# Output projection's second half starts on weights already on chip, chunk norms of the down projection get a PSUM bank, convolution state stored in one piece

## The chip, the cores and the metric

The kernel runs on one core of a Trainium2 chip. A core has five engines that run their own instruction queues and wait for each other through semaphores: TensorE (PE, matrix products into eight PSUM banks), VectorE (DVE), ScalarE (ACT), GpSimd (POOL) and SyncE (SP, which here only issues DMAs; ACT issues some too). The metric is the device time of one launch in microseconds, the median of several runs.

## The reference, cut to what matters

One layer of a streaming encoder on 1024 prompt frames and 8 x 16 sample frames, 1152 columns in the kernel, all in fp32:

```
mix = concat(hgrn2(h), mla(h))          # h: modulated RMSNorm of x
x2  = x + gate1 * (mix @ w_out)         # output projection, 1024 -> 1024
h2  = rmsnorm(x2) * (1 + scale2) + shift2
a, v = split(h2 @ w_up)                 # two branches of D_FF = 2816
a   = causal_conv3(a)                   # its last two rows per sequence: new_state_ffn_conv
x3  = x2 + gate2 * ((gelu(a) * v) @ w_down)
y   = rmsnorm(x3) * gain
```

scale, shift and gate come from a conditioning vector: one for the prompt's columns, one per sequence for the 128 sample columns.

## The kernel before

Activations lie transposed: 128 channels on the partitions, frames along the free axis. Where full fp32 is wanted, a product is made of three (`mm3`, L293 to L295) from a rounded part and a rest of each operand; the rounding is an ACT copy (L288) and the rest a DVE subtraction (L289).

The program is written phase by phase, but a scheduler (the Tile framework) fixes each engine's order at build time by priorities, and adds the semaphore waits. Buffers are named slabs: `B0` to `B11` (128 x 1152 fp32), `W` (128 x 1024, weights), `U` (split parts), each waiting for its last reader when it is written again. `mm` and `bg` are tags of four PSUM banks each. Background pieces of work are generators in a list; `step(n)` advances them by n steps, so their instructions are placed between those of the phase in front.

*Output projection* (`proj_out`). The 1152 columns are two halves (hf) of 576. In each half eight blocks d of 128 output channels are computed in two column pieces c of 288. A piece is 24 products into one `mm` bank, in a half 384 products. The bank is read by `residual`: L1362 adds gate times product to x for the prompt columns; L1365 and L1366 do it for the 128 sample columns, which lie in the second piece of the second half. x comes by L1273 into a slab that holds blocks k and k + 4 side by side; in both halves these are `B4` to `B7`. The weights of a block come by `out_weights`: a load on SP (L1244), the rounding on ACT (L1246), the rest on DVE (L1247, 7/8 of the columns) and POOL (L1248, 1/8), into one of two slots that alternate. In the queue of blocks 0 to 7 stands twice. Then x2 is stored, its squares (L1284) are summed on DVE (L1286, tile `st`).

*Second norm* (`norm2`, once for each half). Two products with ones (L1308) give the sums, L299 to L303 1/sqrt; L1322 multiplies each slab; ACT scales and shifts the prompt columns (L1328); L1331 and L1332 do so for the sample columns on DVE. From the results seven forms (FB11, FB21 ...) are made by subtractions and split, which `up_pair` multiplies: seven products of halves in place of eight. The first norm runs beside the second half of the projection, the second after it.

*Up* (`ffn`, `up_pair`). 22 pairs j with 168 products (L1445) each. ACT (L1448, L1486) and DVE (L1453, L1481) take the banks, e is the gate branch, v the other, and their product g goes to DRAM (gd, L1519). The convolution state of each pair is collected by POOL in `sout` and `tail` and stored by two DMAs on ACT's queue (L1423, L1424).

*Down* (`down`). Three column pieces (704:1152, 256:704, 0:256). In each, all eight d accumulate in all eight banks over 22 j; weights (L1540) and g (L1546) are loaded in 11 steps jp and split. For the last steps d runs outside: then come `residual`, the square (L1575), the sum (L1577). `final` makes the last norm of a piece in the background: the product with ones (L1601) into an `mm` bank, L1602, L299 to L303, the multiplications on POOL (L1609) and DVE (L1611), and the store of y. It yields before it asks for the bank, and all banks are taken by the next piece.

Of the kernel before, what the change touches and what calls it, by code (L numbers as in the profile page):

```python
# [12 lines left out]
F32 = mybir.dt.float32  # L13
# [184 lines left out]
class Layer:  # L198
# [1006 lines left out]
    def phase_c(self):  # L1205
        nc = self.nc
        self.mla_in()
        soft, turned = None, None
        for pr in range(2):
            K, V = self.keys(pr)  # L1210
            if pr == 1:
                self.bg.append(self.sample_mla())
            for i in range(2):
                h = 2 * pr + i
                for pj in range(4):
                    Ps = self.scores(h, pj, K[i])
                    if turned:
                        self.values(*turned)
                    turned = soft and (soft[0], soft[1], self.weights_t(soft[1], soft[2]), soft[3])
                    soft = (h, pj, Ps, V)  # L1220
                    self.step(2)
        self.values(*turned)
        self.queue, self.ahead, self.n_out = list(range(KT)) * 2, [], 0
        self.out_weights()
        self.values(soft[0], soft[1], self.weights_t(soft[1], soft[2]), soft[3])
# [36 lines left out]
    def x2_slab(self, hf, k):  # L1262
        return self.B(4 + k).rearrange("p (two n) -> p two n", two=2)

    def proj_out(self, hf, ms, steps):
        nc = self.nc
        n = 2 * HALF
        base = n * hf
        st = self.B(10).rearrange("p (two n) -> p two n", two=2) if hf == 0 else self.u([P, 2, n], s="st")
        acc, sq = st[:, 0], st[:, 1]  # L1270
        for d in range(KT):
            x2 = self.x2_slab(hf, d % 4)[:, d // 4]
            nc.sync.dma_start(x2, self.I["x"][d, :, base:base + n])  # L1273
            self.out_weights()
            w = self.ahead.pop(0)
            self.out_weights()
            for c in (slice(0, HALF), slice(HALF, n)):
# [5 lines left out]
            nc.scalar.dma_start(self.x2d[d][:, base:base + n], x2)  # L1283
            nc.scalar.activation(sq if d else acc, x2, AF.Square)  # L1284
            if d:
                nc.vector.tensor_add(acc, acc, sq)  # L1286
# [12 lines left out]
    def norm2(self, hf, acc, forms):  # L1299
        nc = self.nc  # L1300
        n = 2 * HALF
        base = n * hf
        rv = self.B(11).rearrange("p (two n) -> p two n", two=2) if hf == 0 else self.u([P, 2, n], s="rv")
        r, v = rv[:, 0], rv[:, 1]
# [5 lines left out]
        yield  # L1310
        self.rstd(r, v, acc)
        yield
# [6 lines left out]
        b12, b11, b22, b21 = bs  # L1319
        for k in range(4):  # L1320
            x = xs[k]
            nc.vector.tensor_mul(x, x, r.unsqueeze(1).to_broadcast([P, 2, n]))  # L1322
            for i, outs in enumerate(((b12, b11), (b22, b21))):
                d = k + 4 * i
                for c, o in enumerate(outs):
# [3 lines left out]
                    if m < HALF:  # L1329
                        y, z = [a.rearrange("p (b t) -> p b t", t=DS) for a in (x[:, i, HALF * c + m:HALF * c + HALF], o[:, k, m:])]  # L1330
                        nc.vector.tensor_mul(z, y, self.smod(SC2, d))  # L1331
                        nc.vector.tensor_add(z, z, self.smod(SH2, d))  # L1332
            yield
# [24 lines left out]
    def residual(self, x2, p, d, lo, m):  # L1358
# [4 lines left out]
        if k < n:  # L1363
            t = self.tmp()
            nc.vector.tensor_mul(t.rearrange("p (b t) -> p b t", t=DS), p[:, k:n].rearrange("p (b t) -> p b t", t=DS), self.smod(m, d))  # L1365
            nc.vector.tensor_add(x2[:, k:], x2[:, k:], t)  # L1366

# [47 lines left out]
    def ffn(self):  # L1415
        nc = self.nc
        self.gd = [self.dp.tile([P, T], F32, name=self.name("gd")) for _ in range(NFF)]
        sin, sout = [self.s([P, NFF, NB, 2]) for _ in range(2)]
        tail = self.s([P, NFF, 2])
        nc.sync.dma_start(sin, self.I["st_c"])  # L1420
        for j in range(NFF):
            self.up_pair(j, sin, sout, tail)
        nc.scalar.dma_start(self.O["cv_o"][:, :, :NB], sout)  # L1423
        nc.scalar.dma_start(self.O["cv_o"][:, :, NB], tail)  # L1424
        self.down()

    def up_pair(self, j, sin, sout, tail):
        nc, V = self.nc, self.vec
        e = self.slab("B", (1, 3)[j % 2], F32)
        c, v = self.slab("B", 2, F32), self.B(0)  # L1430
        nc.gpsimd.memset(e[:, :2], 0.0)
# [77 lines left out]
        nc.gpsimd.tensor_copy(sout[:, j], e[:, SEQ:SEQ + 18 * 8].rearrange("p (n c) -> p n c", c=18)[:, :, :2])  # L1509
        nc.gpsimd.tensor_copy(tail[:, j], e[:, EXT - 2:])  # L1510
        w = [V[:, V_CW + NFF * i + j:V_CW + NFF * i + j + 1] for i in range(3)]
# [10 lines left out]
    def down(self):  # L1522
# [7 lines left out]
        wraw = [self.B(10, DM), self.B(11, DM)] + [self.W(i, F32) for i in range(4)]  # L1530
        graw = [self.B(1, 896)] + [self.W(i, F32, 896) for i in (4, 5)]

# [19 lines left out]
        for ci, c in enumerate((slice(704, T), slice(256, 704), slice(0, 256))):  # L1552
            n = c.stop - c.start
            last = c.start == 0
            x2 = [two(self.B(((4, 5, 6, 7), (0, 3, 2, 8))[ci % 2][d // 2], 896))[:, d % 2, :n] for d in range(KT)]
# [36 lines left out]
    def final(self, c, x2, parts, v, r):  # L1592
# [3 lines left out]
        l = parts[0]  # L1596
        if not last:
            yield
        p = self.ps()[:, :n]
# [36 lines left out]
```

## Time and profile before

| | |
|---|---|
| median of 3 runs | 1571.71 us (1570.76 to 1573.54) |
| the profiled execution's own time | 1573.41 us |
| its span in the trace | 1571.6 us |
| mean granted clock of TensorE in it | 0.978 |
| busy: PE, DVE, ACT, POOL | 1488.8, 977.7, 694.0, 205.4 us |
| share of the chain that ended last: PE, DVE, DMA, ACT | 62%, 4%, 2%, 2% |

The profiled execution is 1.70 us slower than the median; sums are made against it. Idle time of an engine counts only where the end hangs on it; in the list of waits a line says which engine waited at which line for whom.

### The profile page before, as it was taken

Reading aid. Unit: us, or ns where it says so; the run is one execution under the profiler, and the core shown is the slowest. Engines: PE = TensorE matmul, PEld = TensorE weight load, DVE = VectorE, ACT = ScalarE, POOL = GpSimd, SP = SyncE. Lnnn points to the kernel's source line nnn. Section 1 sums busy time; section 2 is a strip of 40 time slices with the busy share of each in tenths; the row PEclk is TensorE's granted clock in tenths of the full one; section 3 lists DMA queues with packets and bytes.
Section 4 is the critical chain, followed back from the end, with each engine's and each line's share of the span. In section 5 each row is a group of like instructions: output and inputs, shape, how many; then the busy total and the mean of one; then the engine's idle time right before and its main releaser. Section 6 shows DMA issues by size and latency. Waiting matters only on the chain.

```text
span 1571.6 us, 28482 instructions
## 1 busy us (share of the span) xinstructions
PE 1488.8 (95%) x11756; PEld 1383.9 (88%) x11756; DVE 977.7 (62%) x1566; ACT 694.0 (44%) x1233; POOL 205.4 (13%) x195
## 2 busy tenths in 40 slices
PE   6999999999999999998699999999999989999996
PEld 4897779998888877788599999999999979999995
DVE  5677666496768665378866666566656553453565
ACT  4453435353446554354544444444444443242451
POOL 1223232332251000011000000000000000000002
PEclk8999999999999999999799999999999999999998
DMA  9234541112120448653022122212221497454552
GB/s 330 97 125 153 185 147 52 57 65 69 59 87 18 159 167 288 236 190 124 26 69 80 63 84 78 75 59 84 84 71 58 136 241 270 141 168 145 170 191 74
DMA packets 77730, 195.47 MB, mean 124 GB/s; under 512 B 13792, under 2 KB 35936, under 8 KB 77600
## 3 DMA queue, kind: packets, MB, share of 16 engines
q1 hardware_dynamic: 60912, 166.67, 31.9%
q10 hardware_dynamic: 16688, 26.98, 4.9%
q8 instruction: 92, 1.51, 0.4%
q14 instruction: 38, 0.31, 0.1%
HBM read 160.68 MB, written 31.17 MB: 122 GB/s over the span
## 4 chain that ended last, share of the span: by engine, by line
PE 62%; DVE 4%; DMA 2%; ACT 2%; issue 1%; SPq 0%; DVEq 0%; ACTq 0%
PE mm L1445 18%; PE bg L1445 13%; PE mm L293 5%; PE mm L295 5%; PE mm L294 5%; PE bg L294 3%; PE bg L295 3%; PE bg L293 3%; PE bg L1139 2%; DMA W<-in_w_down 1%; PE bg L1182 1%; DMA B<-in_x 1%; PE mm L1047 0%; PE mm L1048 0%; PE mm L1050 0%
## 5 line engine op out<-in xcount | busy, mean ns | idle before, releaser
L1445 PE MATMUL mm<-U,W 128*128 128x288 f32 x1848 | 261.1, 297 | 13.4 <-ACT U L288 11.1
L1445 PEld LDWEIGHTS mm<-U,W 128*128 128x128 f32 x1848 | 251.5, 189 | 15.7 <-ACT U L288 11.4
L1445 PE MATMUL bg<-U,W 128*128 128x288 f32 x1320 | 189.4, 297 | 1.6 <-DVE B L1481 1.2
L1445 PEld LDWEIGHTS bg<-U,W 128*128 128x128 f32 x1320 | 181.5, 190 | 2.5 <-DVE B L1481 1.4
L289 DVE TENSOR_TENSOR W<-B,W 128x512 fp32r<-128x512 f32 (+1 forms) x132 | 102.7, 780 | 107.5 <-ACT W L288 104.9
L288 ACT CAST W<-B 128x512 fp32r<-128x512 f32 (+1 forms) x132 | 91.1, 693 | 148.1 <-PE mm L1445 46.6
L293 PE MATMUL mm<-hh,w 128*128 128x384 f32 x432 | 150.3, 348 | 0.0
L294 PE MATMUL mm<-hl,w 128*128 128x384 f32 x432 | 146.6, 339 | 2.0 <-DVE hl L486 2.0
L295 PE MATMUL mm<-hh,w 128*128 128x384 f32 x432 | 146.2, 338 | 0.0
L289 DVE TENSOR_TENSOR U<-W,U 128x1024 fp32r<-128x1024 f32 (+2 forms) x66 | 72.5, 1129 | 87.5 <-ACT U L288 85.9
L288 ACT CAST U<-W 128x1024 fp32r<-128x1024 f32 (+2 forms) x66 | 62.0, 972 | 98.9 <-PE bg L294 80.1
L293 PE MATMUL mm<-U,U 128*128 128x448 f32 (+1 forms) x264 | 90.4, 342 | 6.4 <-ACT B L1486 6.4
L293 PE MATMUL bg<-U,U 128*128 128x448 f32 (+1 forms) x264 | 89.7, 340 | 0.0
L294 PE MATMUL bg<-U,U 128*128 128x448 f32 (+1 forms) x264 | 89.7, 340 | 0.0
L295 PE MATMUL bg<-U,U 128*128 128x448 f32 (+1 forms) x264 | 89.5, 339 | 0.0
L295 PE MATMUL mm<-U,U 128*128 128x448 f32 (+1 forms) x264 | 89.5, 339 | 0.0
L294 PE MATMUL mm<-U,U 128*128 128x448 f32 (+1 forms) x264 | 89.5, 339 | 0.0
L293 PEld LDWEIGHTS mm<-hh,w 128*128 128x128 f32 x432 | 81.9, 190 | 8.1 <-issue 7.4
L1448 ACT COPY B<-mm 128x288 f32<-128x288 f32 x132 | 51.7, 394 | 79.3 <-PE mm L1445 63.1
L293 PE MATMUL mm<-mh,W 128*128 128x288 f32 x256 | 77.5, 304 | 8.8 <-DVE s L1365 5.2
L294 PEld LDWEIGHTS mm<-hl,w 128*128 128x128 f32 x432 | 82.1, 190 | 3.5 <-DVE hl L486 2.3
L295 PEld LDWEIGHTS mm<-hh,w 128*128 128x128 f32 x432 | 82.0, 190 | 0.8 <-issue 0.8
(408 smaller groups left out, 3343.7 us busy)
## 6 DMA issues: line engine op xcount, KB each, us to landing
wa<-in_w_ada SPq DMA_DIRECT2D x48, 512.0 KB, 7.4
B<-in_w_up SPq DMA_DIRECT2D x44, 512.0 KB, 3.3
W<-in_w_down SPq DMA_DIRECT2D x44, 512.0 KB, 4.0
gd<-B ACTq DMA_DIRECT2D x22, 576.0 KB, 2.8
B<-in_w_down SPq DMA_DIRECT2D x22, 512.0 KB, 3.5
w<-in_w_in SPq DMA_DIRECT2D x18, 512.0 KB, 3.6
lT<-in_latT SPq DMA_DIRECT2D x16, 512.0 KB, 8.3
ln<-in_lat SPq DMA_DIRECT2D x16, 512.0 KB, 6.1
```

The lines of the kernel that those rows point to most:

```text
L288: self.nc.scalar.copy(hi, raw)
L289: self.nc.vector.tensor_sub(lo, raw, hi.bitcast(F32))
L293: mm(out, lhsT=w[0], rhs=x[0], start=start, stop=False)
L294: mm(out, lhsT=w[0], rhs=x[1], start=False, stop=False)
L295: mm(out, lhsT=w[1], rhs=x[0], start=False, stop=stop)
L1139: mm(d[64 * j:64 * j + 64, :w], lhsT=q, rhs=ks[j][c], start=c == 0, stop=c == 2, tile_position=(0, 64 * j))
L1182: mm(po[64 * j:64 * j + 64, :KVL], lhsT=PT[:, k, 64 * j:64 * j + 64], rhs=rhs, start=k == 0, stop=k == NT - 1, tile_position=(0, 64 * j))
L1445: nc.tensor.matmul(out, lhsT=l[:, k], rhs=x[:, k], start=start and k == 0 and i == 0, stop=stop and k == 3 and i == 2, skip_group_check=True)
L1448: nc.scalar.copy(t[:, h], X[h][:, :HALF])
```

## The change

It touches four places.

1. *Output projection, second half.* The order of the blocks becomes 6, 7, 0 to 5. Blocks 6 and 7 use the two weight slots that the first half left (`kept`), so 14 blocks are loaded and split in place of 16. The slabs of x2 in this half are `B6`, `B7` and two new tiles (`x2`), which the first half doesn't use; the other buffers move with them. norm2 takes the slabs in the order 2, 3, 0, 1. The add for the sample columns (L1366 before, L1376 now; 8 times) and norm2's multiply and add for them (L1331 and L1332 before, L1341 and L1342 now; 16 times) go from DVE to POOL.
2. *Last up pair.* v is written to `B1`, not `B0`; the first g of down goes to `B0`, not `B1`.
3. *Convolution state.* One tile, one store.
4. *Down.* Only seven blocks of a piece take a bank at once (`bg` for d under 4, then three of `mm`). Block 7 gets its bank after the first two steps jp, and then does its products of these four j. `final` asks for its bank at once; it is advanced by two steps after the first jp, by one after the second.

```diff
-        self.queue, self.ahead, self.n_out = list(range(KT)) * 2, [], 0
+        self.queue, self.ahead, self.kept, self.n_out = list(range(KT)) + list(range(KT - 2)), [], [], 0
...
     def x2_slab(self, hf, k):
-        return self.B(4 + k).rearrange("p (two n) -> p two n", two=2)
+        if hf == 1 and k > 1:
+            if k not in self.x2_more:
+                self.x2_more[k] = self.u([P, 2, 2 * HALF], s="x2")
+            return self.x2_more[k]
+        return self.B((4, 6)[hf] + k).rearrange("p (two n) -> p two n", two=2)
...
-        st = self.B(10).rearrange("p (two n) -> p two n", two=2) if hf == 0 else self.u([P, 2, n], s="st")
+        st = self.B((10, 8)[hf]).rearrange("p (two n) -> p two n", two=2)
...
-        for d in range(KT):
+        self.x2_more, kept = {}, self.kept
+        order = ((0, 1, 2, 3, 4, 5, 6, 7), (6, 7, 0, 1, 2, 3, 4, 5))[hf]
+        for i, d in enumerate(order):
             x2 = self.x2_slab(hf, d % 4)[:, d // 4]
             nc.sync.dma_start(x2, self.I["x"][d, :, base:base + n])
-            self.out_weights()
-            w = self.ahead.pop(0)
-            self.out_weights()
+            if hf and i < 2:
+                w = kept[i]
+            else:
+                w = self.ahead.pop(0)
+            if i < KT - 1 if hf == 0 else i:
+                self.out_weights()
+            self.kept = self.kept[-1:] + [w]
...
-        for k in range(4):
+        for k in (2, 3, 0, 1):
...
-                        nc.vector.tensor_mul(z, y, self.smod(SC2, d))
-                        nc.vector.tensor_add(z, z, self.smod(SH2, d))
+                        nc.gpsimd.tensor_mul(z, y, self.smod(SC2, d))
+                        nc.gpsimd.tensor_add(z, z, self.smod(SH2, d))
...
-            nc.vector.tensor_add(x2[:, k:], x2[:, k:], t)
+            (nc.gpsimd if m == G1 else nc.vector).tensor_add(x2[:, k:], x2[:, k:], t)
...
-        nc.scalar.dma_start(self.O["cv_o"][:, :, :NB], sout)
-        nc.scalar.dma_start(self.O["cv_o"][:, :, NB], tail)
+        nc.scalar.dma_start(self.O["cv_o"], sout)
...
-        c, v = self.slab("B", 2, F32), self.B(0)
+        c, v = self.slab("B", 2, F32), self.B(0 if j < NFF - 1 else 1)
...
-        graw = [self.B(1, 896)] + [self.W(i, F32, 896) for i in (4, 5)]
+        graw = [self.B(0, 896)] + [self.W(i, F32, 896) for i in (4, 5)]
...
-            pd = [self.ps("mm" if d < 4 else "bg") for d in range(KT)]
+            pd = [self.ps("bg" if d < 4 else "mm") for d in range(KT - 1)]
...
-            for jp in range(NFF // 2 - LAST):
+            first = [a for jp in range(2) for a in load(jp, c)]
+            for j, w, g in first[:2]:
+                for d in range(KT - 1):
+                    mult(d, j, w, g)
+            self.step(2)
+            for j, w, g in first[2:]:
+                for d in range(KT - 1):
+                    mult(d, j, w, g)
+            pd.append(self.ps("mm"))
+            for j, w, g in first:
+                mult(KT - 1, j, w, g)
+            self.step(1)
+            for jp in range(2, NFF // 2 - LAST):
...
         l = parts[0]
-        if not last:
-            yield
         p = self.ps()[:, :n]
```

How the queues stand at three places. First SP's queue around the second half of the projection, before (`W` is a raw weight buffer, `B` from `in_x` a slab of x2, `B` from `in_w_up` a weight of the up projection):

```order
L1244 DMA W986_6696<-in_w_out 128x1024
L1273 DMA B1020_6799<-in_x 128x576 x2
L1273 DMA B1046_6925<-in_x 128x576
L1390 DMA B1112_7544<-in_w_up 128x1024
L1244 DMA W1021_6801<-in_w_out 128x1024
L1273 DMA B1056_7030<-in_x 128x576
L1273 DMA B1046_6925<-in_x 128x576
L1273 DMA B1079_7154<-in_x 128x576
L1273 DMA B1056_7030<-in_x 128x576
L1273 DMA B1079_7154<-in_x 128x576
```

The loads of x stand close together: three ahead of the third-last weight load, five behind it. Now:

```order
L1279 DMA x21134_7591<-in_x 128x576 x2
L1399 DMA B1019_6798<-in_w_up 128x1024
L1244 DMA W986_6696<-in_w_out 128x1024
L1279 DMA B1056_7030<-in_x 128x576 x2
L1279 DMA B1079_7154<-in_x 128x576
L1400 DMA B1112_7540<-in_w_up 128x1024
L1244 DMA W1021_6801<-in_w_out 128x1024
L1279 DMA B1079_7154<-in_x 128x576
L1244 DMA W986_6696<-in_w_out 128x1024
L1279 DMA x21138_7654<-in_x 128x576 x2
L1244 DMA W1021_6801<-in_w_out 128x1024
```

The first slab (x21134, of blocks 6 and 2) stands ahead of a weight load for block 0; the slab of blocks 7 and 3 (x21138) is the last of the four, behind two more weight loads.

Second, the second norm of the second half, DVE before (`rv` is 1/sqrt, `nb` a result, `c4` the modulation):

```order
L303 SCALAR_TENSOR_TENSOR rv1162_8134<-st1133_7594,rv1162_8134 128x576
L1322 TENSOR_TENSOR B1020_6799<-B1020_6799,rv1162_8134 128x1152
L1322 TENSOR_TENSOR B1046_6925<-B1046_6925,rv1162_8134 128x1152
L1331 TENSOR_TENSOR nb1179_8160<-B1020_6799,c4_72 128x128
L1331 TENSOR_TENSOR nb1181_8162<-B1020_6799,c4_72 128x128
L1332 TENSOR_TENSOR nb1179_8160<-nb1179_8160,c4_72 128x128
L1332 TENSOR_TENSOR nb1181_8162<-nb1181_8162,c4_72 128x128
L1331 TENSOR_TENSOR nb1179_8160<-B1046_6925,c4_72 128x128
L1331 TENSOR_TENSOR nb1181_8162<-B1046_6925,c4_72 128x128
```

Now DVE has the four multiplications in a row, and POOL the sample columns:

```order
L303 SCALAR_TENSOR_TENSOR B1132_7569<-B1131_7568,B1132_7569 128x576
L1332 TENSOR_TENSOR x21134_7591<-x21134_7591,B1132_7569 128x1152
L1332 TENSOR_TENSOR x21138_7654<-x21138_7654,B1132_7569 128x1152
L1332 TENSOR_TENSOR B1056_7030<-B1056_7030,B1132_7569 128x1152
L1332 TENSOR_TENSOR B1079_7154<-B1079_7154,B1132_7569 128x1152
```

```order
L1440 COPY B1130_7567<-s1205_8232 128x8x2
L1440 COPY B1132_7569<-s1205_8232 128x8x2
L1341 TENSOR_TENSOR nb1180_8153<-x21134_7591,c4_72 128x128
L1342 TENSOR_TENSOR nb1180_8153<-nb1180_8153,c4_72 128x128
L1341 TENSOR_TENSOR nb1182_8155<-x21134_7591,c4_72 128x128
L1342 TENSOR_TENSOR nb1182_8155<-nb1182_8155,c4_72 128x128
L1341 TENSOR_TENSOR nb1180_8153<-x21138_7654,c4_72 128x128
L1341 TENSOR_TENSOR nb1182_8155<-x21138_7654,c4_72 128x128
L1342 TENSOR_TENSOR nb1180_8153<-nb1180_8153,c4_72 128x128
```

The sixteen sample operations left DVE and stand on POOL behind two copies. On TensorE 60 products of the up projection now stand between the norm's products with ones and the first product that needs the form FB11; before it was 36.

Third, the end of the last piece of down on DVE, before (`W1366` is 1/sqrt of the piece before, `bg` and `mm` are banks):

```order
L1362 SCALAR_TENSOR_TENSOR B1346_13030<-mm1376_14444,c4_72,B1346_13030 128x256
L1602 TENSOR_SCALAR W1366_13736<-mm1384_14568 128x448
L1362 SCALAR_TENSOR_TENSOR B1346_13030<-mm1377_14445,c4_72,B1346_13030 128x256
L301 TENSOR_TENSOR B1158_8116<-W1366_13736 128x448
L1362 SCALAR_TENSOR_TENSOR B1347_13031<-mm1378_14446,c4_72,B1347_13031 128x256
L302 SCALAR_TENSOR_TENSOR B1158_8116<-W1366_13736,B1158_8116 128x448
L303 SCALAR_TENSOR_TENSOR W1366_13736<-B1158_8116,W1366_13736 128x448
L1362 SCALAR_TENSOR_TENSOR B1347_13031<-mm1379_14447,c4_72,B1347_13031 128x256
L1611 SCALAR_TENSOR_TENSOR B1129_7570<-B1129_7570,c1_69,W1366_13736 128x448
L1611 SCALAR_TENSOR_TENSOR B1131_7572<-B1131_7572,c1_69,W1366_13736 128x448
L1577 TENSOR_TENSOR B1158_8116<-B1158_8116 128x256
L1362 SCALAR_TENSOR_TENSOR B1348_13032<-bg1380_14448,c4_72,B1348_13032 128x256
```

Now:

```order
L1372 SCALAR_TENSOR_TENSOR B1345_13020<-bg1375_14434,c4_72,B1345_13020 128x256
L1372 SCALAR_TENSOR_TENSOR B1345_13020<-bg1376_14435,c4_72,B1345_13020 128x256
L1598 TENSOR_TENSOR B1160_8110<-B1160_8110 128x256
L1372 SCALAR_TENSOR_TENSOR B1346_13021<-bg1377_14436,c4_72,B1346_13021 128x256
L1598 TENSOR_TENSOR B1160_8110<-B1160_8110 128x256
L1372 SCALAR_TENSOR_TENSOR B1346_13021<-bg1378_14437,c4_72,B1346_13021 128x256
```

The norm of the piece before (L1602, L301 to L303, L1611) is gone from among the residuals; it now stands at the start of the piece, as the same norm of the first piece does in the second.

## Rows read from the trace of the kernel before

**Rows 1.** Page, part 1: busy us (share of the span) and instructions of each engine
```profile
PE 1488.8 (95%) x11756; PEld 1383.9 (88%) x11756; DVE 977.7 (62%) x1566; ACT 694.0 (44%) x1233; POOL 205.4 (13%) x195
```

**Rows 2.** Waits of PE: engine, line, waited for; us, times, longest us
```profile
PE mm L1445 <- ACT U L288: 11.1, 1, 11.1
...
PE mm L293 <- ACT B L1486: 6.4, 1, 6.4
...
PE mm L1601 <- DVE B L1577: 5.1, 1, 5.1
...
PE bg L1445 <- DVE B L1481: 1.2, 1, 1.2
```

**Rows 3.** Timeline of PE, output projection's second half: start, duration, instruction, [idle before]
```profile
702.04 0.61 PE L293 MATMUL mm<-mh,W 128*128 128x288 f32 x1 [3.54 <-DVE B L1362]
...
705.30 0.29 PE L294 MATMUL mm<-ml,W 128*128 128x288 f32 x1
...
724.82 0.58 PE L293 MATMUL mm<-mh,W 128*128 128x288 f32 x1 [5.19 <-DVE s L1365]
...
729.23 0.30 PE L293 MATMUL mm<-mh,W 128*128 128x288 f32 x1
```

**Rows 4.** Timeline of DVE there
```profile
701.46 0.52 DVE L1362 SCALAR_TENSOR_TENSOR B<-mm,c,B 128x288 f32<-128x288 f32 x1 [1.74 <-DMA B<-in_x]
...
724.39 0.28 DVE L1365 TENSOR_TENSOR s<-mm,c 128x128 f32<-128x128 f32 x1
```

**Rows 5.** Stretch, with busy us of PE, PEld, DVE, ACT, POOL; granted clock; DMA
```profile
720.00:730.00 10.00, 5.18 (x24) 5.21 (x25) 9.62 (x14) 4.04 (x4) 0.20 (x2) 0.66 0.25 84
```

**Rows 6.** Timelines of PE, DVE and ACT, second norm of the second half
```profile
754.84 4.30 PE L1445 MATMUL bg<-U,W 128*128 128x288 f32 x24
...
759.79 2.63 DVE L1322 TENSOR_TENSOR B<-B,rv 128x1152 f32<-128x1152 f32 x2
...
769.08 3.24 ACT L288 CAST U<-nb 128x1152 fp32r<-128x1152 f32 x3
```

**Rows 7.** Timeline of POOL: its subtraction for the weights, without and with DVE beside it
```profile
700.19 0.45 POOL L1248 TENSOR_TENSOR W<-W,W 128x128 fp32r<-128x128 f32 x1 [6.49 <-ACT W L1246]
711.19 1.52 POOL L1248 TENSOR_TENSOR W<-W,W 128x128 fp32r<-128x128 f32 x1 [10.54 <-ACT W L1246]
```

**Rows 8.** Timelines of ACT and PE, start of down
```profile
1271.19 0.94 ACT L288 CAST U<-W 128x896 fp32r<-128x896 f32 x1 [6.75 <-DMA W<-gd]
...
1275.12 0.39 ACT L1486 COPY B<-mm 128x288 f32<-128x288 f32 x1
...
1275.56 0.74 PE L293 MATMUL mm<-U,U 128*128 128x448 f32 x1 [6.37 <-ACT B L1486]
...
1278.71 0.37 PE L295 MATMUL bg<-U,U 128*128 128x448 f32 x1
```

**Rows 9.** Waits of SP's queue, 1225 to 1330 us
```profile
SPq L1546 <- DMA out_cv_o<-s: 11.7, 2, 6.9
```

**Rows 10.** DMA issues: KB each, median us from issue to landing
```profile
s<-in_st_c SPq DMA_DIRECT2D x1, 176.0 KB, 3.9
out_cv_o<-s ACTq DMA_DIRECT2D x1, 176.0 KB, 12.2
```

**Rows 11.** Timelines of PE, DVE, POOL and ACT, end of the last piece
```profile
1549.83 2.97 DVE L1611 SCALAR_TENSOR_TENSOR B<-B,c,W 128x448 f32<-128x448 f32 x2
...
1558.76 0.48 DVE L1362 SCALAR_TENSOR_TENSOR B<-bg,c,B 128x256 f32<-128x256 f32 x1
...
1549.66 7.99 POOL L1609 TENSOR_TENSOR B<-B,W 128x448 f32<-128x448 f32 x6 [292.63 <-DVE W L303]
...
1559.78 0.42 ACT L1575 ACTIVATE B<-B 128x256 f32<-128x256 f32 x1 [0.49 <-DVE B L1577]
...
1559.80 2.07 PE L1601 MATMUL mm<-B,c 128*128 128x256 f32 x4 [5.07 <-DVE B L1577]
```

**Rows 12.** Stretch at the end, columns as in rows 5
```profile
1560.00:1571.00 11.00, 1.88 (x4) 0.98 (x4) 5.17 (x9) 1.03 (x3) 2.60 (x3) 0.50 0.29 96
```

More of the change, by code (lines that the diff above doesn't have):

```diff
@@ L1283, in proj_out @@
             nc.scalar.dma_start(self.x2d[d][:, base:base + n], x2)
-            nc.scalar.activation(sq if d else acc, x2, AF.Square)
-            if d:
+            nc.scalar.activation(sq if i else acc, x2, AF.Square)
+            if i:
                 nc.vector.tensor_add(acc, acc, sq)
@@ L1302, in norm2 @@
         base = n * hf
-        rv = self.B(11).rearrange("p (two n) -> p two n", two=2) if hf == 0 else self.u([P, 2, n], s="rv")
+        rv = self.B((11, 3)[hf]).rearrange("p (two n) -> p two n", two=2)
         r, v = rv[:, 0], rv[:, 1]
@@ L1310, in norm2 @@
         yield
-        self.rstd(r, v, acc)
+        self.rstd(r, v, acc if hf == 0 else self.B(2, n))
         yield
@@ L1417, in ffn, with up_pair @@
         self.gd = [self.dp.tile([P, T], F32, name=self.name("gd")) for _ in range(NFF)]
-        sin, sout = [self.s([P, NFF, NB, 2]) for _ in range(2)]
-        tail = self.s([P, NFF, 2])
+        sin, sout = self.s([P, NFF, NB, 2]), self.s([P, NFF, 9, 2])
         nc.sync.dma_start(sin, self.I["st_c"])
         for j in range(NFF):
-            self.up_pair(j, sin, sout, tail)
-        nc.scalar.dma_start(self.O["cv_o"][:, :, :NB], sout)
-        nc.scalar.dma_start(self.O["cv_o"][:, :, NB], tail)
+            self.up_pair(j, sin, sout)
+        nc.scalar.dma_start(self.O["cv_o"], sout)
         self.down()
-    def up_pair(self, j, sin, sout, tail):
+    def up_pair(self, j, sin, sout):
         nc, V = self.nc, self.vec
         e = self.slab("B", (1, 3)[j % 2], F32)
-        c, v = self.slab("B", 2, F32), self.B(0)
+        c, v = self.slab("B", 2, F32), self.B(0 if j < NFF - 1 else 1)
         nc.gpsimd.memset(e[:, :2], 0.0)
@@ L1508, in up_pair @@
                     more()
-        nc.gpsimd.tensor_copy(sout[:, j], e[:, SEQ:SEQ + 18 * 8].rearrange("p (n c) -> p n c", c=18)[:, :, :2])
-        nc.gpsimd.tensor_copy(tail[:, j], e[:, EXT - 2:])
+        nc.gpsimd.tensor_copy(sout[:, j, :NB], e[:, SEQ:SEQ + 18 * 8].rearrange("p (n c) -> p n c", c=18)[:, :, :2])
+        nc.gpsimd.tensor_copy(sout[:, j, NB], e[:, EXT - 2:])
         w = [V[:, V_CW + NFF * i + j:V_CW + NFF * i + j + 1] for i in range(3)]
@@ L1554, in down @@
             last = c.start == 0
-            x2 = [two(self.B(((4, 5, 6, 7), (0, 3, 2, 8))[ci % 2][d // 2], 896))[:, d % 2, :n] for d in range(KT)]
-            pd = [self.ps("mm" if d < 4 else "bg") for d in range(KT)]
+            x2 = [two(self.B(((4, 5, 6, 7), (1, 3, 2, 8))[ci % 2][d // 2], 896))[:, d % 2, :n] for d in range(KT)]
+            pd = [self.ps("bg" if d < 4 else "mm") for d in range(KT - 1)]
             def mult(d, j, w, g):
                 self.mm3(pd[d][:, :n], [a[:, P * d:P * d + P] for a in w], g, j == 0, j == NFF - 1)
-            for jp in range(NFF // 2 - LAST):
+            first = [a for jp in range(2) for a in load(jp, c)]
[11 more added lines that the diff above has]
+            for jp in range(2, NFF // 2 - LAST):
                 for j, w, g in load(jp, c):
```

## The prediction

> **What bounds the kernel now.** I read the page first, then the list of PE's waits, then the timeline around each wait. The page has PE busy for 1488.8 us, 95% of the span [rows 1], while DVE, ACT and POOL have room. So a gain can only come from the stretches in which PE stands still, or from the two ends. The list of waits [rows 2] says where PE stands still late in the program; it is read with its last column, the longest single wait. Four places bear on this change: the output projection's second half, the second norm behind it (11.1 us for the cast of FB11), the start of down (6.4 us) and the last norm (5.1 us).
>
> In the projection's second half PE waits twice for an `mm` bank [rows 3]: 3.54 us before the product at 702.04, because the residual that empties the bank waited for x to land [rows 4], and 5.19 us at 724.82, because L1365 stood on DVE behind the first norm's splits [rows 4]. After each wait PE runs slowly for a while: the stretch from 720 to 730 us has a granted clock of 0.66 [rows 5], between the two levels of 1.2 and 2.4 GHz. Half of a slow stretch is lost: (705.30 - 702.04) / 2 = 1.6 us and (729.23 - 724.82) / 2 = 2.2 us [rows 3]. So this half loses 3.5 + 1.6 + 5.2 + 2.2 = 12.5 us.
>
> At the start of down PE waits 6.37 us for L1486, a copy that takes a bank of the last up pair [rows 8]. The copy lasts 0.39 us, but stands on ACT behind casts, and one of these waited 6.75 us for a load of g [rows 8]. That load stood on SP's queue, which waited 11.7 us in two waits for the store of the convolution state [rows 9]: 176 KB that take 12.2 us to land [rows 10]. The slow stretch behind it costs (1278.71 - 1275.56) / 2 = 1.6 us [rows 8].
>
> At the end, the norm of the second piece runs among the residuals of the third: two multiplications take DVE 2.97 us from 1549.83, and six take POOL 7.99 us [rows 11]. The last residual then runs at 1558.76, though the last product ended at 1559.80 - 5.07 = 1554.73 [rows 11].
>
> **The change part by part.** Sums are made against the profiled execution, 1573.41 us.
>
> *Projection.* Two loads, casts and subtractions of weights go; they lay beside PE's work and are priced at nothing. What counts is the x loads. The slab of blocks 6 and 2 is a new tile and its load stands early on SP, so the residual of the first two pieces waits for no x: the first wait goes, 3.5 + 1.6 = 5.1 us. The slab of blocks 7 and 3 is loaded behind two weight loads, each of which waits until L1247 has read the buffer, and L1247 shares DVE with the splits. Its two banks are then held as the bank at 724.82 is held now. Bounds: nothing of the second loss stays (gain 12.5), or the wait for x merely moves to block 7 and both stay (gain 0, and at worst a longer hold, -2). I take it that one wait of the present second one's size stays, now for block 7, because the order leaves the residual behind the same splits: gain 5.1 us.
>
> *Second norm.* Before, DVE starts multiplying at 759.79 and ACT casts FB11 at 769.08 [rows 6]: 9.3 us. Now DVE does four multiplications in a row (1.3 us each, 2.63 for two [rows 6]) and POOL sixteen sample operations. POOL's price for 128x128 is 0.45 us alone and 1.52 us beside a DVE operation [rows 7]. Only the first four can meet DVE's multiplications: 1.3 + 4 x 1.52 + 12 x 0.45 = 12.8 us, that is 3.5 us later. But 60 products stand ahead of that wait and not 36, and 24 such products take 4.3 us here [rows 6]. So the wait starts later by about as much as it ends later: 0, with bounds of +1 and, if all sixteen cost 1.52 us, 1.3 + 24.3 - 9.3 - 4.3 = -12. The eight adds of the residual that go to POOL delay the sums of squares by one operation at the end; I take 0.5 us off: gain 4.6 for both.
>
> The Trainium skill ("SBUF — State Buffer", section "SBUF: two separate sides") says that DVE and GpSimd share a pair of ports by an exclusive lock: whichever instruction starts first holds it to its end, and the other is blocked. The rows agree (1.52 against 0.45 us), and the rule speaks against moving elementwise work to POOL. By it, too, only operations that meet a running DVE instruction pay, so here it gives the same sum, unless something keeps DVE running beside all sixteen: that is a rival below.
>
> *Start of down.* One store of 128 rows replaces thousands of short ones. Its price isn't in the trace; the nearest row is the load of the state, the same 176 KB in 128 rows, 3.9 us [rows 10]; the other end is 12.2 us. I take 3.9: the shape decides, and the rows differ in that. The 11.7 us of SP's wait then fall to a few, the loads of g arrive under the last up pair's products, and the copy doesn't queue behind a starved cast. v in `B1` also frees the last pair from the store of the pair before it, the 1.2 us for L1481 [rows 2]. Gain 6.4 + 1.6 + 1.2 = 9.2 us; bounds 3 (loads still late by 5 us and more) and 11.
>
> *Norms of the pieces.* At the start of a piece the norm's product stands behind the first 42 products (two j, seven blocks, three each), and 42 more follow before block 7 needs a bank. A product of this shape takes 0.2 us at full clock (half of 3.15 us for eight [rows 8]), so L1602 has 42 x 0.2 = 8.4 us to read the norm's bank, and DVE is not near its limit. I price both starts at nothing; if that cover is gone, PE waits for every microsecond that L1602 comes later. At the end, DVE and POOL are free of the second piece's norm. The last residual (0.48) and square (0.42 [rows 11]) follow the last product, so the product with ones starts near 1554.73 + 0.1 + 0.48 + 0.1 + 0.42 = 1555.8 and not at 1559.80: 4.0 us. It lasts 2.07 us [rows 11] at a granted clock of 0.50 [rows 12]; with a wait of one microsecond ahead of it the clock may stay up, which gives 0 to 1.0 us; I take 0.5. Gain 4.5, bounds 3 and 5.
>
> *Sum.* 4.6 + 9.2 + 4.5 = 18.3 us: 1573.41 - 18.3 = 1555.1. The profiled execution lies 1.70 us above the median of the runs, so against that median the forecast is **1553.4 us**.
>
> **The rivals.**
> 1. *The x load of block 7 eats the projection's gain.* For it: the order of SP's queue, and the 1.74 us that DVE already stands waiting for x [rows 4]; all that is behind it on DVE, splits and weights among it, waits too. Against: only three weight loads stand between it and the first slab's load on SP. The 5.1 us go: 1558.5.
> 2. *The start of down stays bound by loads.* Without the store SP still has to bring weights and g for two steps through few buffers. For it: DMA waits are all along ACT's casts there [rows 8]. Gain there 3 in place of 9.2: 1559.6.
> 3. *POOL becomes the second norm's bound.* At a price c for each of the sixteen the wait ends 1.3 + 16c - 9.3 - 4.3 = 16c - 12.3 us later than forecast. At 1.52 us [rows 7] that is 12.0: 1565.4. It ends **slower than before** by over 0.2% once 16c - 12.3 exceeds 18.3 + 3.1, so from c = 2.1 us; at 2.3 us it gives 24.5 more, 1577.9. For it: each add waits for its own multiplication, and an operation there can lose to DVE as at 711.19 [rows 7]. Against: no row for this size is above 1.52.
> 4. *The projection loses both waits*, since slabs and weights are early: another 7.4 us, 1546.0. Against: the order, as said.
> That the change doesn't do what it says I can exclude: the orders show the weights kept, one store, and the norms moved.
>
> **How the numbers follow.** Forecast 0.57, rival 1 0.15, rival 2 0.10, rival 4 0.06; rival 3 0.12, of which 0.05 with operations up to 1.52 us, 0.03 with some 1.9 (16 x 1.9 - 12.3 = 18.1, all of the gain) and 0.04 from 2.1 on. 0.2% is 3.1 us, about what the measurement can tell from no change. Faster by more than that: 0.57 + 0.15 + 0.10 + 0.06 + 0.05 = 0.93; same 0.03; slower 0.04. The forecast's own range is 1550 to 1557, from the bounds of the last norm (3 to 5), the start of down and the second norm (0 to +1). The range for 8 in 10 reaches to rivals 1 and 2 and a little below the forecast's own: 1548 to 1561; rivals 3 and 4, 0.18 together, lie outside.
>
> **What would show it.** Right, if in the profile after: PE's list of waits has no 3.5 us wait for L1362, but one of 3 to 7 us in the projection's second half; the wait for FB11's cast is still 10 to 12 us, now behind POOL; nothing above 1.5 us stands between 1230 and 1300 us, with the store landing within 6 us; L1620, as the product with ones is now called, waits about a microsecond at the end. Wrong, if the wait for the cast exceeds 15 us, if POOL's L1341 and L1342 lie above 1 us each, if SP still waits for the state's store, or if PE waits at the start of a piece for block 7's bank.

## The result, and the profile after

The changed kernel takes 1555.47 us (median of 4 runs, 1554.28 to 1557.15) where the kernel before takes 1572.62 (median of 4, 1570.76 to 1576.03): ratio 0.9889, 95% interval 0.9868 to 0.991, 17 us. Forecast were 1553.4 us and 18.3 us of gain.

The profiled execution after took 1556.36 us (span 1554.5, granted clock 0.983). The waits of PE in it, from 680 us on, in the same form as [rows 2]; lines are shifted, so that L1372 answers to L1362, L1453 to L1445, L1620 to L1601:

```profile
PE mm L1453 <- ACT U L288: 9.6, 1, 9.6
PE mm L293 <- DVE x L1372: 3.4, 1, 3.4
PE bg L1318 <- DVE B L1296: 2.9, 1, 2.9
PE mm L1453 <- ACT B L1456: 1.4, 2, 0.9
PE mm L293 <- DVE B L1372: 1.3, 1, 1.3
...
PE mm L1620 <- ACT B L1596: 0.3, 1, 0.3
```

The waits of 6.4 us at the start of down and of 5.1 us at the end are gone, those of the projection's second half went from 3.5 and 5.2 to 1.3 and 3.4 us, and the wait for FB11 is 9.6 us where it was 11.1. The wait for the sums of squares (L1296) grew; before, it was

```profile
PE bg L1308 <- DVE st L1286: 2.3, 1, 2.3
```

Spans of two executions can't simply be subtracted here: the same instructions ahead of the projection took 596.1 us in the profile before and 600.8 us in the one after. So I count from the projection's first product. Two profiles of each kernel give these stretches (first product of a stretch to that of the next; both profiles, then the difference of the means):

| stretch | before | after | gain | forecast |
|---|---|---|---|---|
| up to the projection's first product | 596.1, 599.9 | 600.8, 598.9 | scatter | 0 |
| projection, first half | 88.4, 89.4 | 89.0, 88.5 | 0.1 | 0 |
| projection, second half | 64.6, 63.7 | 59.5, 59.8 | 4.5 | 5.1 |
| second norm and first two up pairs | 66.8, 66.9 | 65.4, 65.3 | 1.5 | -0.5 |
| further up pairs, to the 3600th product | 435.3, 435.3 | 435.0, 435.0 | 0.3 | 0 |
| end of up, 47 products of down | 33.6, 33.3 | 24.1, 24.2 | 9.3 | 9.2 |
| rest of down | 269.7, 269.7 | 269.2, 269.2 | 0.5 | 0 |
| last product to the end | 17.1, 17.1 | 11.5, 11.5 | 5.6 | 4.5 |

From the projection on the change is worth 975.44 - 953.67 = 21.8 us, means of two profiles each. Two profiles are few for the middle rows: of the experiments below, those with the old code in a stretch took 63.7 to 64.6 us for the second half (four profiles, mean 64.1) and 65.8 to 66.9 for the norm (66.5), those with the new 57.8 to 59.8 (seven, 58.9) and 63.1 to 65.8 (six, 64.9), with nearly the same waits. By these means the gains are 5.2 and 1.6 us.

The projection, second half, timeline of PE in the changed kernel (answers to [rows 3]):

```profile
714.46 0.40 PE L293 MATMUL mm<-mh,W 128*128 128x288 f32 x1 [1.29 <-DVE B L1372]
...
721.32 0.58 PE L293 MATMUL mm<-mh,W 128*128 128x288 f32 x1 [3.43 <-DVE x L1372]
...
726.91 0.30 PE L295 MATMUL mm<-mh,W 128*128 128x288 f32 x1
```

and of DVE, with the residual of block 7 at 720.66:

```profile
712.41 1.57 DVE L289 TENSOR_TENSOR U<-B,U 128x1152 fp32r<-128x1152 f32 x1
713.90 0.50 DVE L1372 SCALAR_TENSOR_TENSOR B<-mm,c,B 128x288 f32<-128x288 f32 x1
...
715.60 2.61 DVE L289 TENSOR_TENSOR U<-B,U 128x1152 fp32r<-128x1152 f32 x2
718.13 1.34 DVE L1356 TENSOR_TENSOR B<-B,B 128x1152 f32<-128x1152 f32 x1
719.40 1.34 DVE L1247 TENSOR_TENSOR W<-W,W 128x896 fp32r<-128x896 f32 x1
720.66 0.80 DVE L1372 SCALAR_TENSOR_TENSOR x<-mm,c,x 128x288 f32<-128x288 f32 x2
```

The residual has no idle time ahead of it: what it waits for is DVE's turn. With the slow stretch behind it (granted clock 0.51 from 721.3 to 726.9 us) the half still loses 1.3 + 3.4 + (726.91 - 721.32) / 2 = 7.5 us.

The second norm, timelines of DVE, POOL, ACT and PE (answers to [rows 6, 7]):

```profile
761.27 2.63 DVE L1332 TENSOR_TENSOR x<-x,B 128x1152 f32<-128x1152 f32 x2
763.82 3.04 DVE L1332 TENSOR_TENSOR B<-B,B 128x1152 f32<-128x1152 f32 x2
...
762.80 1.36 POOL L1341 TENSOR_TENSOR nb<-x,c 128x128 f32<-128x128 f32 x1 [1.51 <-DVE x L1332]
764.24 1.40 POOL L1342 TENSOR_TENSOR nb<-nb,c 128x128 f32<-128x128 f32 x1
765.60 1.51 POOL L1341 TENSOR_TENSOR nb<-x,c 128x128 f32<-128x128 f32 x1
767.20 0.40 POOL L1342 TENSOR_TENSOR nb<-nb,c 128x128 f32<-128x128 f32 x1
...
771.16 0.76 POOL L1342 TENSOR_TENSOR nb<-nb,c 128x128 f32<-128x128 f32 x2
...
771.60 1.15 ACT L288 CAST U<-nb 128x1152 fp32r<-128x1152 f32 x1 [1.38 <-POOL nb L1342]
...
772.80 3.54 PE L1453 MATMUL mm<-U,W 128*128 128x288 f32 x13 [9.58 <-ACT U L288]
```

Three operations met DVE's multiplications and cost 1.4 to 1.5 us, the thirteen others about 0.36 us each. The last ends at 771.92, 0.9 us ahead of the product with FB11 at 772.80: POOL is now what the cast waits for.

The start of down has no row above 0.9 us; the one store of 198 KB lands after 5.4 us, and SP doesn't wait for it. DMA issues (answers to [rows 10]):

```profile
out_cv_o<-s ACTq DMA_DIRECT2D x1, 198.0 KB, 5.4
```

What the two stores did before shows in the loads beside them. DMA in the kernel before, 1259 to 1269 us, and in the changed one, 1256 to 1262 us; `W<-gd` are two loads of g issued in that time, in KB each and median us to landing:

```profile
DMA packets 4248, 0.91 MB, mean 91 GB/s; under 512 B 3887, under 2 KB 4216, under 8 KB 4248
...
W<-gd SPq DMA_DIRECT2D x2, 224.0 KB, 10.7
```

```profile
DMA packets 801, 2.05 MB, mean 342 GB/s; under 512 B 80, under 2 KB 464, under 8 KB 800
...
W<-gd SPq DMA_DIRECT2D x2, 224.0 KB, 5.4
```

The end, timelines of PE, ACT and DVE (answers to [rows 11]):

```profile
1542.98 0.28 PE L295 MATMUL mm<-U,U 128*128 128x256 f32 x1
1543.37 0.70 PE L1620 MATMUL mm<-B,c 128*128 128x256 f32 x2
1544.35 0.70 PE L1620 MATMUL mm<-B,c 128*128 128x256 f32 x2 [0.27 <-ACT B L1596]
...
1543.30 0.48 DVE L1372 SCALAR_TENSOR_TENSOR B<-mm,c,B 128x256 f32<-128x256 f32 x1
...
1543.88 0.42 ACT L1596 ACTIVATE B<-B 128x256 f32<-128x256 f32 x1 [1.02 <-DVE B L1372]
```

Residual and square now follow the last product directly; two of the four products with ones run ahead of them, and each pair takes 0.70 us where four took 2.07.

### The profile page after: what moved, and what is told of

Its sections match the earlier page's. It is cut to its first block, busy times and chain, and to the rows that moved or that the text cites. A ratio compares the mean times of both kernels' runs of the same rounds, so it can differ in the third digit from the quotient of the medians.

```text
span 1554.5 us, 28456 instructions
## 1 busy us (share of the span) xinstructions
PE 1489.3 (96%) x11756; PEld 1386.5 (89%) x11756; DVE 974.1 (63%) x1540; ACT 690.5 (44%) x1231; POOL 225.7 (15%) x217
## 4 chain that ended last, share of the span: by engine, by line
PE 85%; DVE 7%; ACT 3%; issue 2%; DMA 2%; POOL 1%; SPq 0%; ACTq 0%; DVEq 0%; POOLq 0%
PE mm L1453 18%; PE bg L1453 13%; PE mm L293 11%; PE mm L294 11%; PE mm L295 11%; PE bg L294 3%; PE bg L295 3%; PE bg L293 3%; PE bg L1139 2%; PE bg L381 1%; PE bg L708 1%; PE bg L1182 1%; DVE sl L800 1%; DMA wa<-in_w_ada 1%; PE bg L791 1%
## 5 line engine op out<-in xcount | busy, mean ns | idle before, releaser
L1453 PE MATMUL mm<-U,W 128*128 128x288 f32 x1848 | 260.8, 296 | 11.5 <-ACT U L288 9.6
L1453 PEld LDWEIGHTS mm<-U,W 128*128 128x128 f32 x1848 | 251.5, 189 | 13.3 <-ACT U L288 9.8
L1453 PE MATMUL bg<-U,W 128*128 128x288 f32 x1320 | 189.3, 297 | 0.0
L1453 PEld LDWEIGHTS bg<-U,W 128*128 128x128 f32 x1320 | 181.7, 190 | 0.3
L289 DVE TENSOR_TENSOR W<-B,W 128x512 fp32r<-128x512 f32 (+1 forms) x132 | 102.5, 780 | 106.7 <-ACT W L288 104.5
L293 PE MATMUL mm<-hh,w 128*128 128x384 f32 x432 | 152.7, 353 | 0.0
L295 PE MATMUL mm<-hh,w 128*128 128x384 f32 x432 | 149.0, 345 | 0.0
L289 DVE TENSOR_TENSOR U<-W,U 128x1024 fp32r<-128x1024 f32 (+2 forms) x66 | 74.9, 1167 | 70.4 <-ACT U L288 70.3
```

Of the source, the lines that this page charges most:

```text
L289: self.nc.vector.tensor_sub(lo, raw, hi.bitcast(F32))
L293: mm(out, lhsT=w[0], rhs=x[0], start=start, stop=False)
L295: mm(out, lhsT=w[1], rhs=x[0], start=False, stop=stop)
L1453: nc.tensor.matmul(out, lhsT=l[:, k], rhs=x[:, k], start=start and k == 0 and i == 0, stop=stop and k == 3 and i == 2, skip_group_check=True)
```

## The experiments

The theory: the three places are separate, and each gain is a wait that goes. Rivals: the parts lean on each other; something else at each place does it. Twelve kernels ran, four on one chip at a time; a ratio is to the kernel before on that chip. "From the projection on" is the time from its first product to the end: 975.4 us before, 953.7 after.

**The changed kernel and the kernel before once more.** 

> The changed kernel once more, on the chip of the runs beside it. Theory (the parts add up): ratio to before 0.985 to 0.989; from the projection's first product to the end 21 to 22 us less than the kernel before's profile. Rival (the first measurement of 0.989 is all there is, the parts take from each other): 0.989 or above.

> The kernel before once more, for a second profile. Theory (the time up to the projection's first product scatters by some 6 us between executions of the same instructions, and says nothing of the change): that product starts between 594 and 601 us, and from it to the end it takes 975 us, within 3 us. Rival (the changed program slows its own beginning by 3 to 4 us): it starts at 596 us within 1 us again.

No edit. After: ratio 0.9884 (0.9857 to 0.991), 953.6 us from the projection on. Before: 1.0006 (0.9995 to 1.0018), 975.4 us, with its first product at 599.9 us. Both theories held, the first at the edge. Over all fourteen profiles the projection's first product starts between 594.9 and 600.8 us, on either side of the change; a difference of 4.6 us there says nothing of it. The table above uses these two profiles as its second numbers.

**The store alone.** 

> Kernel before with the convolution state in one tile and one store, nothing else. Theory (the store held SP's loads of g, and these ACT's bank copy): the store lands in about 5.4 us as in the changed kernel, SP's wait for it (11.7 us) goes, PE's 6.4 us wait at the start of down falls below 1.5 us, gain about 8 us (ratio 0.995); the 1.2 us wait for L1481 stays. Rival (v in B1 does it, the store only stands beside): a wait of 4 us or more stays there, gain at most 3 us.

```diff
-        nc.scalar.dma_start(self.O["cv_o"][:, :, :NB], sout)
-        nc.scalar.dma_start(self.O["cv_o"][:, :, NB], tail)
+        nc.scalar.dma_start(self.O["cv_o"], sout)
```

Ratio 0.9921 (0.9905 to 0.9938), 12.5 us, more than the 8 expected; 964.8 us from the projection on, 10.6 less. (The diff leaves out the copies that fill the one tile.) The store landed after 5.9 us, the two loads of g after 3.7 and 5.0, SP waited for the store no more, and the list of PE's waits has one line at the start of down:

```profile
PE mm L1443 <- ACT B L1446: 0.7, 1, 0.7
```

The wait of 1.2 us for L1481, which was expected to stay, is gone too. The rival falls: without v in `B1` and with the old banks, the store explains the whole of that stretch. From the 336th up product to the 48th of down it takes 459.1 us, as the changed kernel does; the kernel before took 468.7 and 468.9.

**The store undone.** 

> Changed kernel with the convolution state again in two tiles and two stores. Theory: SP waits 10 us or more for the store, PE waits 6 to 10 us at the start of down, 8 to 12 us slower than the changed kernel. Rival (v in B1 and the new banks cover the store): under 3 us slower.

The same diff reversed, in the changed kernel. Ratio 0.9918 (0.9888 to 0.9948), 1561.56 us beside 1554.63 of the changed kernel on that chip: 6.9 us, less than the 8 to 12 expected. The end of up and the start of down take 34.0 us where the changed kernel takes 24.1, so there the size was as forecast. From the projection on it is 962.7 us, 9.0 more; 2.1 of these are slow products of down (last section), and the stretches up to the 336th up product were 3.3 us shorter. The longer store took 17.3 us to land, and PE waited for a cast:

```profile
PE bg L293 <- ACT U L288: 8.6, 1, 8.6
```

Of SP's waits only 3.5 us carry the store's name and not 10 or more: that detail was wrong. Timeline of ACT:

```profile
1251.48 10.61 ACTq L1434 DMA_DIRECT2D out_cv_o<-s  x1
1262.19 0.94 ACT L288 CAST U<-B 128x896 fp32r<-128x896 f32 x1 [10.37 <-DMA W<-in_w_down]
```

The issue of the second store (8 B runs, 22 KB) lasts 10.61 us on ACT's queue, where the one store of the changed kernel takes 0.34, and the cast starts 0.10 us behind it. The profile names a load of weights for the cast's wait, but the g that it casts had landed by 1251.72. So this wait of PE comes from ACT's queue and not from SP's.

**v in `B0`.** 

> Changed kernel with the last up pair's v in B0 again and the first g of down in B1. Theory: the last pair waits 1 to 1.5 us for the store of the pair before (L1489 or the bank behind it), 1 to 1.5 us slower than the changed kernel, no other wait. Rival (v's place decides the start of down): a wait of 4 us or more there.

```diff
-        c, v = self.slab("B", 2, F32), self.B(0 if j < NFF - 1 else 1)
+        c, v = self.slab("B", 2, F32), self.B(0)
```

(and the two lines that use `B0` and `B1` in down.) The wait came, 1.3 us for L1489, but the run was not slower: 1555.22 us, ratio 0.9867 (0.9852 to 0.9882), 953.0 us from the projection on, of which 1.9 are slow products of down (last section). The scatter can hide 1.3 us. From the 336th up product to the 48th of down it takes 459.7 us where the changed kernel takes 459.1; that v in `B1` gains its 1.2 us is not shown.

**Down's banks alone.** 

> Kernel before with the new banks and steps of down alone. Theory: the wait ahead of the last products with ones falls from 5.1 us to below 1 us and these four products run at full clock, so the time from the last product to the end falls by about 5.6 us and the run by 5 to 6 us (ratio 0.9965); no wait at the start of a piece. Rival (block 7's bank): a wait of 1 us or more at the start of pieces two and three, gain below 3 us.

The changed kernel's `down` and `final` with all else as before. Ratio 0.9964 (0.995 to 0.9977), 5.7 us. That is as forecast, and so are the end, 11.8 us in place of 17.1, and that pieces two and three start without a wait. But the wait at the start of down grew:

```profile
PE bg L293 <- DVE B L1453: 9.0, 1, 9.0
```

where the wait before was 6.4 us: the first products now need `bg` banks, and those are emptied by DVE, which stood behind splits for the same late loads. So from the projection on only 0.7 us were left in the profiled execution (974.8), the slowest of twelve; 1.9 us of slow products of down (last section) are in that.

**Down's banks undone.** 

> Changed kernel with down's banks and the norms' steps as before. Theory: the 5 us wait ahead of the last products with ones is back and the time from the last product to the end is 17 us in place of 11.5; all else stays, 5 to 6 us slower than the changed kernel. Rival (the banks' order at the start of down matters more): the start of down changes by 2 us or more.

The same in reverse, in the changed kernel. Ratio 0.9901 (0.9886 to 0.9916), 4.6 us above v_in_b0 beside it, which ran as the changed kernel does. The wait ahead of the products with ones is back:

```profile
PE mm L1609 <- DVE B L1585: 5.1, 1, 5.1
```

and the end takes 17.2 us. From the projection on it is 961.5, 7.8 more: 5.7 at the end, and 1.6 at the start of down, where PE waited 2.6 us for a copy of `mm`. The theory holds, and the rival's 2 us are not reached; which banks come first matters little once the loads are in time.

**The projection alone.** 

> Kernel before with the projection's part alone (order, slabs, kept weights, POOL). Theory: from the first product of the projection to the 336th of the up projection 5.8 us less than before, of which about 4.4 in the projection; the waits are about 1.3 and 3.4 us in place of 3.5 and 5.2 us; the run 5 to 6 us faster (ratio 0.9965). Rival (the parts lean on each other or the projection's gain is given back in the up pairs): gain below 2 us.

The first part of the change's diff in the kernel before. Ratio 0.9947 (0.9933 to 0.9961), 8.4 us. To the 336th up product it took 212.4 us (219.7 and 219.9 before); the waits are 1.3 and 3.4 us as forecast. What the new slabs, the kept weights and the adds on POOL each do in it was not run apart. In the profiled execution this was lost again: the wait at the start of down was

```profile
PE mm L293 <- ACT B L1496: 9.8, 1, 9.8
```

and products of down ran slower (3.4 us, last section), so that it took 975.7 us in all. The runs say faster; this one execution, the slowest of six, doesn't.

**x earlier.** 

> Changed kernel, with the loads of x for blocks 6, 7, 2 and 3 written ahead of the second half's loop, so that they stand together on SP's queue. Theory (the late x load of block 7 puts its residual behind the splits on DVE): the residuals of block 7 move ahead of the first norm's splits, the 3.4 us wait goes, 3 to 5 us faster than the changed kernel (ratio to before about 0.986). Rival (DVE has too much work there, the load only decides who waits): a wait of 3 us or more turns up for another bank, time as the changed kernel's (0.989).

```diff
+        early = (6, 7, 2, 3) if hf else ()
+        for d in early:
+            nc.sync.dma_start(self.x2_slab(hf, d % 4)[:, d // 4], self.I["x"][d, :, base:base + n])
...
-            nc.sync.dma_start(x2, self.I["x"][d, :, base:base + n])
+            if d not in early:
+                nc.sync.dma_start(x2, self.I["x"][d, :, base:base + n])
```

Ratio 0.9832 (0.9819 to 0.9846), below both intervals of the changed kernel (from 0.9868 and from 0.9857); 951.1 us from the projection on, 2.6 less than after although 2.1 are slow products of down (last section). The residuals of block 7 ran early, yet a wait of 3.2 us turned up for another bank:

```profile
PE mm L293 <- DVE s L1379: 3.2, 1, 3.2
```

The wait is gone for block 7 and back for L1379, a later residual. So the rival told the mechanism, DVE has too much to do there, and the theory the time: the wait of 1.3 us went, and the second half took 55.5 us, below all seven profiles of the changed code (57.8 to 59.8).

**Residuals ahead of the splits.** 

> As x_early, and the residuals of the projection get the scheduler's high priority, so that they stand between the first norm's splits and not behind them. Theory (what is left of the bank wait is the residuals' place on DVE, whatever x does): no wait above 1 us in the projection's second half, 4 to 5 us less there than in x_early (3.2 us wait and the slow clock behind it). Rival (DVE's total work there is the bound): the splits come later instead and the second norm's wait or the first up pairs give it back; under 2 us.

```diff
-                self.residual(x2[:, c], p, d, base + c.start, G1)
+                with self.tc.high_priority():
+                    self.residual(x2[:, c], p, d, base + c.start, G1)
```

PE's waits from the second half on:

```profile
PE bg L1323 <- DVE B L1301: 4.6, 1, 4.6
PE mm L1458 <- ACT U L288: 3.7, 1, 3.7
PE mm L1458 <- ACT B L1461: 3.0, 5, 1.4
PE bg L1458 <- DVE B L1494: 2.2, 1, 2.2
```

No wait is left in the projection; its second half takes 51.9 us, against 55.5 in x_early, 58.9 in the changed code and 64.1 in the old. But the norm and the first two up pairs take 66.7 us against 63.7 in x_early, so 0.7 us of 3.7 are kept to that point. The rival holds: the splits come later, and PE meets them in the norm. The time is 948.4 us from the projection on, 1550.74 us (1545.57 to 1552.68) beside 1554.63 of the changed kernel on that chip, ratio 0.9863 (0.9834 to 0.9891): the interval overlaps that of the changed kernel (0.9857 to 0.991), so by times it is not shown to be faster, nor faster than x_early (0.9832); by its one profile it is 5.3 us faster than the changed kernel.

**The norm's sample operations on DVE.** 

> Changed kernel with the second norm's sixteen sample operations back on DVE, all else as changed. Theory (POOL is the last to feed the cast of FB11: it ends 0.9 us before it, while ACT is long done): the cast comes when ACT is done, some 9.3 us after DVE's first multiplication and not 11.5, so the wait of 9.6 us falls by about 2 us and the run gets 2 us faster. Rival (DVE then is the last, or POOL is no bound): no change within 1 us.

```diff
-                        nc.gpsimd.tensor_mul(z, y, self.smod(SC2, d))
-                        nc.gpsimd.tensor_add(z, z, self.smod(SH2, d))
+                        nc.vector.tensor_mul(z, y, self.smod(SC2, d))
+                        nc.vector.tensor_add(z, z, self.smod(SH2, d))
```

Timelines of DVE, ACT and PE:

```profile
756.57 2.63 DVE L1332 TENSOR_TENSOR x<-x,B 128x1152 f32<-128x1152 f32 x2
...
761.69 0.38 ACT L1456 COPY B<-mm 128x288 f32<-128x288 f32 x1
...
765.85 1.14 ACT L288 CAST U<-nb 128x1152 fp32r<-128x1152 f32 x1
...
762.12 2.34 PE L1453 MATMUL mm<-U,W 128*128 128x288 f32 x12 [3.61 <-ACT B L1456]
```

The cast comes 9.3 us after the first multiplication, as forecast, and PE no longer waits for it; it waits 3.6 us for a copy that stands on ACT between the norm's activations. The norm and the two pairs took 63.6 us; that lies among the 63.1 to 65.8 us of the profiles with POOL, so no gain is shown: 951.7 us from the projection on, 2.0 less than after, and 1554.2 beside 1554.63 us by the runs. The place of the wait was right, its worth stays open.

**All three.** 

> x_early_prio with the second norm's sample operations on DVE. Theory (two separate gains): from the projection's first product to the end 945 to 947 us (x_early_prio 948.4, the changed kernel 953.7), ratio to before about 0.984. Rival (the residuals' place and the norm's operations draw on the same DVE time): 948 us or more.

x_early_prio and norm_on_dve in one. 951.3 us from the projection on, 2.9 more than without the last edit, of which 1.9 are slow products of down (last section); ratio 0.984 (0.9823 to 0.9856). The theory falls: after the second half (51.9 us) the norm and the first pairs take 67.9 us, with two waits of 5.0 us for DVE, more than in any other profile. By the runs it is 1551.74 us (1547.63 to 1552.22), all four below the four of v_in_b0 beside it (1553.59 to 1556.58); its ratio and that of x_early_prio (0.9863) don't tell the two apart.

## Why the prediction was right

*Projection's second half.* Forecast was that the wait for x goes and one wait of the second's size stays, for block 7, because its residual stands behind the splits. 7.4 us (5.2 and 2.2) were to stay, 7.5 did, as 1.3 + 3.4 + 2.8. The gain is 4.5 to 5.2 us where 5.1 was said. It came as two waits and not one: the 1.3 us are for a residual that stands behind a split too (L289 at 712.41 us). x_early and x_early_prio show that the place on DVE, not the load, is what counts: with x early the wait moves, with the residuals first it is gone.

*Second norm.* The row's -0.5 us is 0 for the norm and 0.5 lost by the adds on POOL. The second came as priced: the wait for the sums of squares is 2.9 us and was 2.3. The first was mis-sized: the wait for FB11 is 1.5 us shorter, and the stretch gained 1.5 to 1.6 us, beyond the bound of 1. POOL took 10.7 us from the first multiplication to its last operation, not 12.8, because three operations met DVE and not four, and the others cost 0.36 us and not 0.45. Counted from the first product with ones, the wait began 3.3 us later, with 24 more up products ahead of it, and ended 1.7 us later; forecast were 4.3 and, counted from the first multiplication, 3.5. (Between the products with ones and the wait stand 48 up products and before 24; the other 12 of the 60 and the 36 stand ahead of the products with ones.) The lock of the Trainium skill ("SBUF — State Buffer", section "SBUF: two separate sides") agrees with the rows: 1.4 to 1.5 us while a multiplication ran, 0.36 to 0.40 after. Whether the move to POOL is worth anything is not shown either way: norm_on_dve lies within the scatter of its neighbours, and the 1.2 us that early_prio_dve takes more than x_early_prio in the norm are one profile against one.

*Start of down.* 9.2 forecast, 9.3 found. Price of the one store: 5.4 us, nearer the low end of 3.9 to 12.2. Two steps don't stand. The 1.2 us for v in `B1` is one; the store, priced at 6.4 + 1.6 = 8.0 us, gave 9.7 of that stretch and of the up pairs before it by itself (cv_only), so that the two errors cancel and the closeness is luck. The other is the path from the store to PE. The prediction has the late load of g on SP's queue, behind SP's waits for the store. But SP stood in these waits from 1264.4 to 1269.2 and from 1270.4 to 1277.3 us, and the two loads that the starved cast of [rows 8] waited for had been issued at 1259.35 and 1259.73. They landed 10.0 and 11.4 us later, in flight beside 3887 packets under 512 B, at 91 GB/s in all; in the changed kernel they take 5.3 and 5.5 us, at 342 GB/s, and in cv_only 3.7 and 5.0. So the store slowed loads that were already issued; what SP's own waits added isn't shown.

*Norms of the pieces.* 4.5 forecast, 5.6 found, above the upper bound of 5 that I gave; the clock term was mis-sized. I moved the four products as a block of 2.07 us and allowed at most 1.0 for the clock; in fact two of them no longer wait for the last square at all, and the others ran at full clock (granted 1.00 from 1543 to 1546 us). From the end of the last product (1542.98 + 0.28) to that of the products with ones (1545.05) it takes 1.8 us; before, 1554.73 to 1561.87, 7.1. Block 7's bank cost nothing: no wait above 0.2 us at the start of a piece.

*The sum.* 18.3 forecast, 21.8 from the projection on, 17 us by the medians. The gap between the last two is not fully explained: the early part was 4.6 us later in the one pair of profiles and scatters by 6 us, and 21.8 us of some 1573 would be a ratio of 0.986, just below the interval of the first measurement and inside that of the second. The terms were off by 2.0 (norm), 1.1 (end) and 0.1 to 0.6 us (the others), so that the median comes within 2.1 us of the forecast is in part luck. Of the signs named, two came out milder than said: the wait for FB11 is 9.6 us and not 10 to 12, and L1620 waits 0.3 us and not about one.

## What to carry to other kernels

When a cast or a bank copy is late, follow its queue back to the load, see when that was issued, and what was in flight beside it: a small store of short rows, issued on the way into a new phase, cost more here than any computation that the change moved (9.7 us), and took back in single executions what other edits gained. A bank is held by the place of its reader on an engine's queue; here, loading the reader's other operand earlier moved the longest wait to another bank (3.4 us became 3.2), and putting the readers first made what they overtook the next wait. Compare stretches between the same two instructions, not spans, when parts that nothing touched scatter by more than the edit.

## What was not expected of the hardware

The same instructions ahead of the projection took 594.9 to 600.8 us over fourteen profiles. And the products of down's first two pieces (128x448) follow each other at one of two rates, 0.2027 or 0.2067 us, with no wait among them. The rate changes only where a norm's products with ones stand among them (behind the 570th product of down in the changed kernel). In six of the fourteen profiles hundreds run at the slower one: those up to the products with ones in x_early, two_stores and proj_only (2.1 us in the first two, 3.4 in the third, where they stand behind the 978th), those behind them in norm_only, v_in_b0 and early_prio_dve (1.9 us). The granted clock reads 1.00 at both rates. Sixteen products of x_early, timeline of PE, then seventeen of the changed kernel:

```profile
1299.72 0.37 PE L293 MATMUL mm<-U,U 128*128 128x448 f32 x1
...
1302.82 0.37 PE L293 MATMUL bg<-U,U 128*128 128x448 f32 x1
```

```profile
1299.71 0.36 PE L294 MATMUL bg<-U,U 128*128 128x448 f32 x1
...
1302.95 0.37 PE L295 MATMUL mm<-U,U 128*128 128x448 f32 x1
```

That is 3.10 / 15 = 0.207 and 3.24 / 16 = 0.2025 us from one to the next. What sets this rate stays open; it is no part of the change, but totals from the projection on hold it, so compare those by stretches.
